# Seven block products instead of eight in half of the down projection's row pairs, with the stationary operands kept in DRAM

## The chip, the cores and the metric

The kernel runs on one core of one Trainium2 chip. The metric is the device time of one execution in microseconds; the time before is the median of three runs. One further execution was recorded by the hardware profiler. Engines: PE multiplies matrices, DVE and ACT work elementwise, POOL is a third elementwise engine that also issues some transfers, SP issues the loads and stores.

## The reference, cut to what matters

One layer of an encoder on 256 tokens of width 2048, all in float32: a mixer with two attention branches, then the MLP at its end:

```python
h = rms_norm(x, norm_mlp_pre[l])
u = jnp.square(jax.nn.relu(jnp.einsum('bsd,df->bsf', h, w_up[l])))      # 2048 -> 8192
x = x + rms_norm(jnp.einsum('bsf,fd->bsd', u, w_down[l]), norm_mlp_post[l])   # 8192 -> 2048
```

The change lies in the last line, the down projection: u is 256 x 8192, w_down is 8192 x 2048.

## The kernel before

Every operand of a large product is split into a high part `hi` (the value rounded to the matmul's float32r format) and a low part `lo` (what is left). A product is three matmuls into the same PSUM bank: hi x hi, hi x lo and lo x hi. ACT makes the high part (a cast), DVE the low part (a subtraction). That is `split`, lines 115 and 116, for weights.

Weights are loaded in pieces of 1 MB by SP's queue into the pool `wp`, which has three buffers each for `raw`, `hi` and `lo`. The loads, the splits and the products are written in program order; a scheduler then decides the order on every engine, and semaphores keep it in step.

The up projection (the loop over `cg`, 16 groups of 512 of the 8192 columns) holds the weights stationary and gives u transposed: `u` is [128 columns, 4, 256 tokens] per group. Its evacuation `u_evac` adds two halves (ACT copy, DVE add, lines 254 and 256), takes the maximum with zero and the scale (line 761), and squares (ACT, line 762). Sixteen tiles `u` stay in SBUF, in the pool `pages` (27 pages of 4 KB per partition).

The down projection holds the activations stationary and lets the weights stream. Its 8192 rows are 64 row tiles `k` of 128. For each, `dweight` loads 128 x 2048 weights and splits them in two halves of 1024 columns, and, once in four row tiles, splits the activations `u` (`usplit`, lines 746 and 747). `dmm` (lines 777 to 779) makes the three matmuls for token tile t (2) and column block c (4 of 512 columns); the eight sums `acc` fill all eight PSUM banks during the whole projection:

```python
for k in range(2, NK - LAST):
    w = dweight(k)
    for t in range(2):
        for c in range(4):
            dmm(k, t, c, w)
```

The last three row tiles go token tile by token tile, so that tile 0 is evacuated while tile 1 is still multiplied. The evacuation squares each bank on ACT with a running sum (line 807), multiplies it with the gain on DVE (line 809), then comes the scale (lines 811, 85, and 88 on POOL) and the output pass with the residual (line 816) with a store (line 819).

Of the kernel before, what the change touches and what calls it, by code (L numbers as in the profile page):

```python
# [17 lines left out]
P = 128  # L18
D = 2048
# [19 lines left out]
def encoder_layer(ctx: ExitStack, tc: tile.TileContext, a, out):  # L39
# [6 lines left out]
    tmp = ctx.enter_context(tc.tile_pool(name="tmp", bufs=6))  # L46
    tiny = ctx.enter_context(tc.tile_pool(name="tiny", bufs=8))
    dram = ctx.enter_context(tc.tile_pool(name="dram", bufs=1, space=bass.MemoryType.DRAM))
    mm = ctx.enter_context(tc.tile_pool(name="mm", bufs=NMM, space=PSUM))
# [22 lines left out]
    def along_tokens(r, b, name):  # L72
        """r [P tokens, token tile] as a row of all tokens, on all partitions."""
# [7 lines left out]
    def inv_rms(ss, n, name, r=None):  # L81
        """(ss / n + eps) ** -0.5, per partition."""
# [9 lines left out]
    last_load = [None]  # L92

    def load(src, k0, nk, c0, cw, name):
        """Rows k0*128.. of a weight: [P, nk, cw]."""
        raw = wp.tile([P, nk, cw], F32, tag="raw", name=f"{name}_w")
        view = src[k0 * P : (k0 + nk) * P, c0 : c0 + cw].rearrange("(k p) c -> p k c", p=P)
        last_load[0] = nc.sync.dma_start(raw, view).ins
# [73 lines left out]
    def advance(n):  # L172
        """Trace the next n stages of the attention heads that wait for their turn, and one chore."""
# [9 lines left out]
    def wgroup(src, c0, act, nk, evac, name, first=(), hook=None, mid=None, after={}, k_first=False, inner=None):  # L183
        """out^T of 512 columns: weights stationary. act(k) is [P, hi 256 | lo 256]."""
# [66 lines left out]
    def halves(ps, name):  # L251
        """The sum of the two halves of a bank, in SBUF."""
# [67 lines left out]
    # Position bias: row (h, i) of rpbp holds the bias of row offset i - 3 at column offsets  # L320
    # -63..63. Each is written 64 times at a pitch of 127 and read at a pitch of 126.
# [52 lines left out]
    def product3(ps, stat, s_at, mov, m_at, start, stop):  # L374
        """ps (+)= stat^T @ mov, each given in two parts."""
# [43 lines left out]
    def p_transposed(p, name):  # L419
        """[P queries, (t, keys)] -> [P keys, (key tile, queries)]"""  # L420
# [320 lines left out]
    ust = {}  # L741

    def usplit(i):
        uh = page([P, 4, T], F32R, f"uh{i}")
        ul = page([P, 4, T], F32R, f"ul{i}")
        nc.scalar.copy(uh, uT[i])
        nc.vector.tensor_sub(ul, uT[i], uh.bitcast(F32))
        ust[i] = (uh, ul)
# [6 lines left out]
    uT = []  # L755
    for cg in range(DFF // 512):
# [8 lines left out]
        uT.append(u)  # L765
        if cg == DFF // 512 - 2:
            usplit(0)

    acc = [[bank(f"acc{t}{c}", t * 4 + c >= 8 - NMM) for c in range(4)] for t in range(2)]
    NK = DFF // P  # L770
    LAST = 3
    def dmm(k, t, c, w):
# [100 lines left out]
```

## Time and profile before

| what | value |
|---|---|
| runs | 1397.62 us median of three (1397.48 to 1398.73) |
| profiled execution, span from first to last instruction | 1394.5 us |
| its own time around the span | not given; the median lies 3.1 us above the span |
| PE, DVE, ACT busy | 1374.6, 835.8, 668.7 us |
| down projection, first to last matmul start | 1037.22 to 1385.18 us |
| 64 loads of `w_down`, 1 MB each | 4.9 us from issue to landing (median) |

A row of a group reads: line, engine, operation, output<-inputs, shape, count | busy time, mean ns of one | idle time of the engine just before them and what ended it. A matmul's duration overlaps the next one's; the pace is read from the starts.

### The profile page before, as it was taken

The page shows a single profiled execution, that of the slowest core. Times are in us where ns is not written, and L with a number is a line of the kernel's source. Part 1 is how long each engine was busy: PE and PEld are TensorE (multiplying, and loading weights), DVE is VectorE, ACT ScalarE, POOL GpSimd, SP SyncE. Part 2 cuts the span into 40 slices and gives each one's busy share as a digit, 9 for nine tenths or more (in the row PEclk, how much of TensorE's full clock was granted, in tenths as well). Part 3 has the DMA queues.
Part 4 walks back from the last instruction along what each step waited for, and adds up shares of the span by engine and source line. Part 5 has one row for each costly group of instructions (what it writes and reads, how often), then busy time and mean ns, then how long its engine had stood idle before and what let it go on. Part 6 is the DMA issues. An engine that isn't in the chain of part 4 may idle for free.

```text
span 1394.5 us, 17896 instructions
## 1 busy us (share of the span) xinstructions
PE 1374.6 (99%) x7240; PEld 1177.8 (84%) x7240; DVE 835.8 (60%) x1155; ACT 668.7 (48%) x1023; POOL 7.9 (1%) x19
## 2 busy tenths in 40 slices
PE   7999999999999999999899999999999999999997
PEld 6888888888888888888788888888888888888886
DVE  6868866676656565654755555555575554444445
ACT  7554554545444445543744444444464543334332
POOL 0000000000000000000000000000000000000000
PEclk9999999999999999999999999999999999999999
DMA  9674755564555555675455565656555556555551
GB/s 317 202 214 154 202 177 173 171 191 155 165 205 182 203 181 183 203 279 184 149 182 181 182 193 170 211 170 200 189 196 185 203 186 227 195 187 205 181 199 73
DMA packets 117490, 265.16 MB, mean 190 GB/s; under 512 B 15008, under 2 KB 16288, under 8 KB 109216
## 3 DMA queue, kind: packets, MB, share of 16 engines
q1 hardware_dynamic: 117264, 264.03, 57.3%
q8 instruction: 56, 0.92, 0.3%
q14 instruction: 26, 0.21, 0.0%
q10 hardware_dynamic: 144, 0.01, 0.0%
HBM read 261.92 MB, written 3.92 MB: 191 GB/s over the span
## 4 chain that ended last, share of the span: by engine, by line
PE 98%; DVE 1%; DMA 0%; ACT 0%; SPq 0%; issue 0%; DVEq 0%; POOLq 0%; POOL 0%; ACTq 0%
PE u_p L191 17%; PE u_p L192 9%; PE acc L779 8%; PE acc L778 8%; PE acc L777 8%; PE gb_p L191 4%; PE ga_p L191 4%; PE qa_p L191 2%; PE gb_p L192 2%; PE ga_p L192 2%; PE ka_p L191 2%; PE qn_p L191 2%; PE bb_p L191 2%; PE ba_p L191 2%; PE kn_p L191 2%; PE y_p L229 2%
## 5 line engine op out<-in xcount | busy, mean ns | idle before, releaser
L191 PE MATMUL u_p<-h2T,u_h 128*128 128x512 f32 x1024 | 359.9, 398 | 0.5 <-DVE r_m L85 0.5
L192 PE MATMUL u_p<-h2T,u_l 128*128 128x256 f32 x1024 | 284.3, 280 | 0.0
L116 DVE TENSOR_TENSOR d_l<-d_w,d_h 128x1024 fp32r<-128x1024 f32 x128 | 151.1, 1221 | 164.2 <-ACT d_h L115 163.7
L116 DVE TENSOR_TENSOR u_l<-u_w,u_h 128x1024 fp32r<-128x1024 f32 x128 | 151.1, 1222 | 146.0 <-ACT u_h L115 144.7
L191 PEld LDWEIGHTS u_p<-h2T,u_h 128*128 128x128 f32 x1024 | 192.0, 189 | 45.5 <-DVE r_m L85 0.9
L115 ACT CAST d_h<-d_w 128x1024 fp32r<-128x1024 f32 x128 | 128.3, 1052 | 191.1 <-PE acc L779 187.5
L778 PE MATMUL acc<-d_l,uh 128*128 128x512 f32 x512 | 199.0, 389 | 0.0
L779 PE MATMUL acc<-d_h,ul 128*128 128x512 f32 x512 | 198.9, 389 | 0.0
L777 PE MATMUL acc<-d_h,uh 128*128 128x512 f32 x512 | 198.2, 389 | 0.0
L192 PEld LDWEIGHTS u_p<-h2T,u_l 128*128 128x128 f32 x1024 | 193.8, 189 | 1.3
L115 ACT CAST u_h<-u_w 128x1024 fp32r<-128x1024 f32 x128 | 128.0, 1049 | 123.9 <-PE u_p L191 62.5
L778 PEld LDWEIGHTS acc<-d_l,uh 128*128 128x128 f32 x512 | 96.1, 188 | 20.1
L777 PEld LDWEIGHTS acc<-d_h,uh 128*128 128x128 f32 x512 | 96.1, 188 | 20.0
L779 PEld LDWEIGHTS acc<-d_h,ul 128*128 128x128 f32 x512 | 96.1, 188 | 19.8
L191 PE MATMUL gb_p<-hT,gb_h 128*128 128x512 f32 x256 | 90.4, 398 | 0.0
L191 PE MATMUL ga_p<-hT,ga_h 128*128 128x512 f32 x256 | 90.0, 397 | 0.0
L192 PE MATMUL gb_p<-hT,gb_l 128*128 128x256 f32 x256 | 71.4, 281 | 0.0
L192 PE MATMUL ga_p<-hT,ga_l 128*128 128x256 f32 x256 | 70.3, 280 | 0.0
L191 PEld LDWEIGHTS gb_p<-hT,gb_h 128*128 128x128 f32 x256 | 47.9, 188 | 11.5
L116 DVE TENSOR_TENSOR gb_l<-gb_w,gb_h 128x1024 fp32r<-128x1024 f32 x32 | 37.8, 1221 | 31.1 <-ACT gb_h L115 31.1
L191 PEld LDWEIGHTS ga_p<-hT,ga_h 128*128 128x128 f32 x256 | 47.4, 188 | 10.5
L116 DVE TENSOR_TENSOR y_l<-y_w,y_h 128x1024 fp32r<-128x1024 f32 x32 | 37.9, 1222 | 27.8 <-ACT y_h L115 27.8
(213 smaller groups left out, 2348.1 us busy)
## 6 DMA issues: line engine op xcount, KB each, us to landing
u_w<-in_w_up SPq DMA_DIRECT2D x64, 1024.0 KB, 5.4
d_w<-in_w_down SPq DMA_DIRECT2D x64, 1024.0 KB, 4.9
ga_w<-in_w_in SPq DMA_DIRECT2D x16, 1024.0 KB, 5.2
gb_w<-in_w_in SPq DMA_DIRECT2D x16, 1024.0 KB, 5.2
y_w<-in_w_out SPq DMA_DIRECT2D x16, 1024.0 KB, 5.1
ka_w<-in_w_in SPq DMA_DIRECT2D x8, 1024.0 KB, 6.1
va_w<-in_w_in SPq DMA_DIRECT2D x8, 1024.0 KB, 5.2
qn_w<-in_w_in SPq DMA_DIRECT2D x8, 1024.0 KB, 5.1
```

Of the source, the lines that this page charges most:

```text
L115: nc.scalar.copy(hi[part], raw[part])
L116: nc.vector.tensor_sub(lo[part], raw[part], hi[part].bitcast(F32))
L191: nc.tensor.matmul(ps[b], hi[:, k % 4, cs], mv, start=(k == 0), stop=False)
L192: nc.tensor.matmul(ps[b][:, :T], lo[:, k % 4, cs], mv[:, :T], start=False, stop=(k == nk - 1))
L229: nc.tensor.matmul(ps[t], sh, hi[:, k % 4], start=(k == 0), stop=False)
L777: nc.tensor.matmul(acc[t][c], uh[:, k % 4, ts_], hi[:, 0, cs], start=(k == 0), stop=False)
L778: nc.tensor.matmul(acc[t][c], uh[:, k % 4, ts_], lo[:, 0, cs], start=False, stop=False)
L779: nc.tensor.matmul(acc[t][c], ul[:, k % 4, ts_], hi[:, 0, cs], start=False, stop=(k == NK - 1))
```

## The change

The down projection is cut anew. A *step* is now two row tiles at a distance of 256 rows (`h` = 0, 1) by 1024 columns (half `g`), so that weights form a matrix of 2 x 2 blocks of 128 x 512, and the activations one of 2 x 2 blocks of 128 x 128 (two row tiles by two token tiles). A load is still 1 MB, in rows of 4 KB. The columns are done in two halves one after the other (`for g in range(2)`); each has 16 groups of 512 rows with two steps each (`j` = 0, 1). In a half, eight banks hold four plain sums and four further sums that are recombined at its end.

Steps of odd groups are *plain*: eight block products, 24 matmuls. Steps of even groups use Winograd's form of Strassen's scheme: *seven* products, 21 matmuls, of sums of blocks. DVE makes four sums of activation blocks after each even group of the up projection (`act_sets`) and four sums of weight blocks for each step (`down_weights`: `dt`, lines 826, 828, 829). Of a seven-product step the raw blocks 1 to 3 (`dh`, `dl`, 128 x 1536) and the sums (`eh`, `el`, 128 x 2048) are split, of a plain step the whole (`dh`, `dl`, 128 x 2048). A seven-product step takes two of the three `hi` and `lo` buffers, a plain one takes one.

The activation parts no longer stay in SBUF. `act_sets` stores them to DRAM from POOL's queue (48 stores, 23 MB), and `act_again` loads them in each column half on SP's queue, right behind the first weight load of their group. In names such as `dl031`, `el100` or `bh010` the digits are the half g, the group, and j (for `bh` and `bl`, the loaded activations, the number of the set). The pool `tmp` is closed ahead of the down projection and its space given to the weight sums. The two gain loads `gp2` now stand ahead of the down projection.

The diff, cut to its core:

```diff
-    def dweight(k):
-        if k % 4 == 0 and k // 4 not in ust:
-            usplit(k // 4)
-        return weight(a["w_down"], k, 1, 0, D, f"d{k}")
+    def act_sets(cg, u):
+        srcs = []
+        if seven_of(cg):
+            a11, a21 = u[:, 0:2, :P], u[:, 0:2, P:]
+            a12, a22 = u[:, 2:4, :P], u[:, 2:4, P:]
+            sums = page([P, 4, 2, P], F32, f"sm{cg}")
+            nc.vector.tensor_sub(sums[:, 0], a21, a22)
+            nc.vector.tensor_sub(sums[:, 1], a11, a21)
+            nc.vector.tensor_sub(sums[:, 2], sums[:, 0], a11)
+            nc.vector.tensor_add(sums[:, 3], a12, sums[:, 2])
...
+            for n, part in (("h", hi), ("l", lo)):
+                kd = dram.tile(shape, F32, name=f"keep{n}{cg}{i}", tag=f"keep{n}{cg}{i}")
+                nc.gpsimd.dma_start(kd, part.bitcast(F32))
+                kept[cg, i, n] = (shape, kd)
+    def act_again(cg, g):
...
+                t = page(shape, F32R, f"b{n}{g}{cg}{i}")
+                nc.sync.dma_start(t.bitcast(F32), kd)
...
+    temps.close()
+    down = ctx.enter_context(tc.tile_pool(name="down", bufs=1, reuse_waits="tile"))
+    wd = a["w_down"].rearrange("(g h j p) c -> p h g j c", h=2, j=2, p=P)
+    def down_weights(g, cg, j):
+        raw = wp.tile([P, 4, 512], F32, tag="raw", name=f"dr{g}{cg}{j}")
+        last_load[0] = nc.sync.dma_start(
+            raw.rearrange("p (h b) c -> p h (b c)", h=2),
+            wd[:, :, cg, j, g * 1024 : (g + 1) * 1024],
+        ).ins
+        n = f"{g}{cg}{j}"
+        h1, l1 = wtile("hi", f"dh{n}"), wtile("lo", f"dl{n}")
+        if not seven_of(cg):
+            nc.scalar.copy(h1, raw)
+            nc.vector.tensor_sub(l1, raw, h1.bitcast(F32))
+            return h1, l1
+        t = down.tile([P, 4, 512], F32, tag="t", name=f"dt{n}", bufs=2)
+        nc.vector.tensor_add(t[:, 0:2], raw[:, 1:3], raw[:, 0:1].to_broadcast([P, 2, 512]))
+        nc.scalar.copy(h1[:, 1:4], raw[:, 1:4])
+        nc.vector.tensor_add(t[:, 2], t[:, 0], raw[:, 2])
+        nc.vector.tensor_add(t[:, 3], t[:, 2], raw[:, 3])
+        nc.vector.tensor_sub(l1[:, 1:4], raw[:, 1:4], h1[:, 1:4].bitcast(F32))
+        h2, l2 = wtile("hi", f"eh{n}"), wtile("lo", f"el{n}")
+        nc.scalar.copy(h2, t)
+        nc.vector.tensor_sub(l2, t, h2.bitcast(F32))
+        return h1, l1, h2, l2
...
+        pr.add(0, stat(0, 0), r, 1, last)
+        pr.add(4, stat(1, 0), t, 0, last)
+        pr.add(6, stat(1, 1), t, 1, last)
+        pr.add(5, stat(1, 2), t, 2, last)
+        pr.add(2, stat(1, 3), r, 2)
+        pr.add(1, stat(0, 1), r, 3)
+        pr.add(3, stat(0, 2), t, 3)
...
+            if g == 0:
+                steps += [n0, s0, n1, s1] if b < NG - 2 else [n0, s0, s1, n1]
+            else:
+                steps += [s0, n0, s1, n1]
...
+                if final:
+                    nc.scalar.copy(c11, pr.ps[0])
+                    nc.vector.tensor_add(c12, c11, pr.ps[5])
+                    nc.vector.tensor_add(c21, c12, pr.ps[6])
+                    nc.vector.tensor_sub(c12, pr.ps[4], c12)
+                    nc.vector.tensor_sub(c22, pr.ps[4], c21)
...
+                eight(pr, sets[cg], j, w, which, end)
+                if end:
+                    nc.vector.tensor_add(z, z, pr.ps[i_])
+                    nc.scalar.activation(sq, z, AF.Square, accum_out=ssd[t][:, c : c + 1])
+                    nc.vector.tensor_mul(z, z, gp2[g][:, half * 512 : (half + 1) * 512])
```

What this makes of the order on DVE is seen at three places. First, in the midst of the down projection before, the low parts of one weight load follow each other, with an activation part now and then:

```order
L747 TENSOR_TENSOR ul7_10135<-u7_7501,uh7_10134 128x1024
L116 TENSOR_TENSOR d7_l_9445<-d7_w_9442,d7_h_9444 128x1024 x2
L116 TENSOR_TENSOR d8_l_9481<-d8_w_9478,d8_h_9480 128x1024 x2
L116 TENSOR_TENSOR d9_l_9513<-d9_w_9510,d9_h_9512 128x1024 x2
L747 TENSOR_TENSOR ul8_10267<-u8_7690,uh8_10266 128x1024
```

Now, in the first column half, two pairs of steps (plain steps 050 and 051, seven-product steps 040 and 041):

```order
L826 TENSOR_TENSOR dt040_9790<-dr040_9786 128x1024
L828 TENSOR_TENSOR dt040_9790<-dt040_9790,dr040_9786 128x512
L829 TENSOR_TENSOR dt040_9790<-dt040_9790,dr040_9786 128x512
L822 TENSOR_TENSOR dl050_9755<-dr050_9752,dh050_9754 128x2048
L830 TENSOR_TENSOR dl040_9789<-dr040_9786,dh040_9788 128x1536
L833 TENSOR_TENSOR el040_9797<-dt040_9790,eh040_9796 128x2048
L826 TENSOR_TENSOR dt041_9863<-dr041_9859 128x1024
L828 TENSOR_TENSOR dt041_9863<-dt041_9863,dr041_9859 128x512
L822 TENSOR_TENSOR dl051_9832<-dr051_9829,dh051_9831 128x2048
L829 TENSOR_TENSOR dt041_9863<-dt041_9863,dr041_9859 128x512
L830 TENSOR_TENSOR dl041_9862<-dr041_9859,dh041_9861 128x1536
```

The sums of a seven-product step (826, 828, 829) stand ahead of, or around, the low part of the plain step (822) that PE multiplies before it. Three pairs later in that half have the last sum (829) behind the step's own 128 x 1536 part (830).

Second, at the start of the down projection DVE had these behind the last up group's halves:

```order
L116 TENSOR_TENSOR d0_l_9217<-d0_w_9214,d0_h_9216 128x1024 x2
L116 TENSOR_TENSOR d1_l_9225<-d1_w_9222,d1_h_9224 128x1024 x2
L256 TENSOR_TENSOR up_s_9160<-u15_p0_9018,up_r_9158 128x256
L256 TENSOR_TENSOR up_s_9174<-u15_p1_9019,up_r_9172 128x256
L761 SCALAR_TENSOR_TENSOR up_s_9160<-up_s_9160,r2b_5461 128x256
```

and now, from the last of these halves on (`up_s` of bank 3), it has:

```order
L257 TENSOR_TENSOR up_s_9438<-u15_p3_9257,up_r_9436 128x256
L798 SCALAR_TENSOR_TENSOR up_s_9438<-up_s_9438,r2b_5461 128x256
L826 TENSOR_TENSOR dt000_9506<-dr000_9502 128x1024
L826 TENSOR_TENSOR dt001_9579<-dr001_9575 128x1024
L774 TENSOR_TENSOR al150_9443<-u15_9253,ah150_9442 128x1024
L828 TENSOR_TENSOR dt000_9506<-dt000_9506,dr000_9502 128x512
L828 TENSOR_TENSOR dt001_9579<-dt001_9579,dr001_9575 128x512
L829 TENSOR_TENSOR dt000_9506<-dt000_9506,dr000_9502 128x512
L829 TENSOR_TENSOR dt001_9579<-dt001_9579,dr001_9575 128x512
L833 TENSOR_TENSOR el000_9513<-dt000_9506,eh000_9512 128x2048
```

The low parts for the first two steps are still made ahead of the halves; the sums of the first seven-product step, and with them `el000`, stand behind them.

Third, at the switch between the column halves, where before there was only the row of `d_l` shown above, DVE now has, from the last plain step of the first half (`dl0151`) to the second half's first sums (`el100`) and the emptying of the banks `p01`, `p02`, `p04` to `p06`:

```order
L822 TENSOR_TENSOR dl0151_10584<-dr0151_10581,dh0151_10583 128x2048
L829 TENSOR_TENSOR dt100_10639<-dt100_10639,dr100_10635 128x512
L830 TENSOR_TENSOR dl100_10638<-dr100_10635,dh100_10637 128x1536
L905 TENSOR_TENSOR zw00_10574<-zw00_10574,p05_9465 128x512
L833 TENSOR_TENSOR el100_10646<-dt100_10639,eh100_10645 128x2048
L906 TENSOR_TENSOR zw01_10575<-zw00_10574,p06_9466 128x512
L915 TENSOR_TENSOR zw00_10574<-zw00_10574,p01_9461 128x512
L826 TENSOR_TENSOR dt101_10716<-dr101_10712 128x1024
L907 TENSOR_TENSOR zw00_10574<-p04_9464,zw00_10574 128x512
L908 TENSOR_TENSOR zw01_10575<-p04_9464,zw01_10575 128x512
L822 TENSOR_TENSOR dl110_10681<-dr110_10678,dh110_10680 128x2048
```

Behind these stand a gain (919), a sum (828) and the pass that empties `p02` (915). The emptying of the banks (905 to 908, 915) is woven into the weight parts.

At the end of the second half the same passes follow the last plain step's part, and the output passes of token tile 0 come only after all of them.

More of the change, by code (lines that the diff above doesn't have):

```diff
@@ new lines, in encoder_layer, with __init__, add @@
+    class Products:
+        def __init__(self, name, low):
+            self.ps = [bank(f"{name}{i}", i in low) for i in range(8)]
+            self.begun = set()
+        def add(self, i, stat, w, blk, last=False):
+            (sh, sl), (wh, wl) = stat, w
+            nc.tensor.matmul(self.ps[i], sh, wh[:, blk], start=i not in self.begun, stop=False)
+            self.begun.add(i)
+            nc.tensor.matmul(self.ps[i], sh, wl[:, blk], start=False, stop=False)
+            nc.tensor.matmul(self.ps[i], sl, wh[:, blk], start=False, stop=last)
@@ new lines, in seven, with stat, eight @@
+    def seven(pr, sets, j, w, last):
+        def stat(i, at):
+            return tuple(part[:, at, j] for part in sets[i])
+        r, t = w[:2], w[2:]
+        pr.add(0, stat(0, 0), r, 1, last)
[5 more added lines that the diff above has]
+        pr.add(3, stat(0, 2), t, 3)
+    PLAIN = ((1, 0, 1), (2, 0, 0), (3, 1, 1), (7, 1, 0))
+    def eight(pr, sets, j, w, which, last):
+        i, t, half = PLAIN[which]
+        for k in (0, 2):
+            stat = tuple(part[:, j + k, t * P : (t + 1) * P] for part in sets[0])
+            pr.add(i, stat, w, k + half, last and k == 2)
@@ L798, in encoder_layer @@
         )
[L799 to L809 removed]
+    zw = {}
@@ new lines, in encoder_layer @@
+    ssd = [small(4, f"ssd{t}") for t in range(2)]
+    for g in range(2):
+        steps = []
+        for b in range(0, NG, 2):
+            s0, s1, n0, n1 = (b, 0), (b, 1), (b + 1, 0), (b + 1, 1)
+            if g == 0:
+                steps += [n0, s0, n1, s1] if b < NG - 2 else [n0, s0, s1, n1]
+            else:
+                steps += [s0, n0, s1, n1]
+        pr = Products(f"p{g}", (0, 4, 5, 6))
+        sets = {}
+        for i, (cg, j) in enumerate(steps):
+            end = i == len(steps) - 1
+            w = down_weights(g, cg, j)
+            if cg not in sets:
+                with tc.issue_after(last_load[0]):
+                    sets[cg] = act_again(cg, g)
+            if seven_of(cg):
+                final = not any(seven_of(c) for c, _ in steps[i + 1 :])
+                seven(pr, sets[cg], j, w, final)
+                if final:
+                    for t in range(2):
+                        zw[g, t] = page([P, 2, 512], F32, f"zw{g}{t}")
+                    c11, c12 = zw[g, 0][:, 1], zw[g, 0][:, 0]
+                    c21, c22 = zw[g, 1][:, 1], zw[g, 1][:, 0]
+                    nc.scalar.copy(c11, pr.ps[0])
[3 more added lines that the diff above has]
+                    nc.vector.tensor_sub(c22, pr.ps[4], c21)
+                continue
+            for which in range(4):
+                eight(pr, sets[cg], j, w, which, end)
+                if end:
+                    i_, t, half = PLAIN[which]
+                    z = zw[g, t][:, half]
+                    nc.vector.tensor_add(z, z, pr.ps[i_])
+                    sq = down.tile([P, 512], F32, tag="junk", name=f"jd{g}{which}", bufs=2)
+                    c = g * 2 + half
+                    nc.scalar.activation(sq, z, AF.Square, accum_out=ssd[t][:, c : c + 1])
+                    nc.vector.tensor_mul(z, z, gp2[g][:, half * 512 : (half + 1) * 512])
```

79 lines of the change are left out of this document (31 added, 48 removed).

## The prediction

> **What bounds the kernel now.** I read the page's busy shares and its chain first.
>
> ```profile
> span 1394.5 us, 17896 instructions
> PE 1374.6 (99%) x7240; PEld 1177.8 (84%) x7240; DVE 835.8 (60%) x1155; ACT 668.7 (48%) x1023; POOL 7.9 (1%) x19
> ...
> PE 98%; DVE 1%; DMA 0%; ACT 0%; SPq 0%; issue 0%; DVEq 0%; POOLq 0%; POOL 0%; ACTq 0%
> ```
>
> PE carries 98% of the chain, so only fewer products, or a stall of PE, can move the time much. The stretches of the up projection and of the down projection show what lies beside PE in each:
>
> ```profile
> core 0: us, PE busy (x) PEld busy (x) DVE busy (x) ACT busy (x) POOL busy (x), PEclk, DMA share, GB/s
> 700.00:1030.00 330.00, 330.00 (x1888) 287.52 (x1887) 183.58 (x239) 158.24 (x238) 0.00 (x0) 1.00 0.58 186
> 1040.00:1384.00 344.00, 344.00 (x1519) 284.87 (x1518) 169.07 (x152) 140.80 (x152) 0.54 (x1) 1.00 0.54 185
> ```
>
> In the down stretch DVE is busy for 49% and the DMA engines for 54%, at full clock. The groups from the end of the up projection on give the durations:
>
> ```profile
> L777 PE MATMUL acc<-d_h,uh 128*128 128x512 f32 x512 | 198.2, 389 | 0.0
> L116 DVE TENSOR_TENSOR d_l<-d_w,d_h 128x1024 fp32r<-128x1024 f32 x128 | 151.1, 1221 | 164.2 <-ACT d_h L115 163.7
> L115 ACT CAST d_h<-d_w 128x1024 fp32r<-128x1024 f32 x128 | 128.3, 1052 | 191.1 <-PE acc L779 187.5 <-issue 3.6
> ...
> L816 DVE SCALAR_TENSOR_TENSOR zw<-zw,rd_r,x 128x512 f32<-128x512 f32 x8 | 5.5, 747 | 0.7 <-POOL rd_r L88 0.7
> L809 DVE TENSOR_TENSOR zw<-acc,gp 128x512 f32<-128x512 f32 x8 | 5.3, 688 | 6.2 <-ACT jd L807 5.9
> L807 ACT ACTIVATE jd<-acc 128x512 f32<-128x512 f32 x8 | 4.7, 596 | 9.8 <-PE acc L779 9.7
> L762 ACT ACTIVATE u<-up_s 128x256 f32<-128x256 f32 x8 | 3.2, 419 | 1.7 <-DVE up_s L761 1.7
> L761 DVE SCALAR_TENSOR_TENSOR up_s<-up_s,r2b 128x256 f32<-128x256 f32 x8 | 3.2, 420 | 0.1
> L256 DVE TENSOR_TENSOR up_s<-u_p,up_r 128x256 f32<-128x256 f32 x8 | 3.2, 419 | 0.0
> L254 ACT COPY up_r<-u_p 128x256 f32<-128x256 f32 x8 | 2.9, 368 | 3.4 <-PE u_p L192 3.4
> ...
> L88 POOL TENSOR_TENSOR rd_r<-rd_m,expo 128x1 f32<-128x1 f32 x2 | 1.1, 540 | 689.6 <-DVE rd_m L85 689.6
> ```
>
> PE never idles there (0.0). The 389 ns of a product overlap the next one; the pace stands in the timeline, from the last product of the up projection to the first and the last of the down projection:
>
> ```profile
> 1037.10 0.28 PE L192 MATMUL u_p<-h2T,u_l 128*128 128x256 f32 x1
> 1037.22 0.39 PE L777 MATMUL acc<-d_h,uh 128*128 128x512 f32 x1
> ...
> 1385.18 0.39 PE L779 MATMUL acc<-d_h,ul 128*128 128x512 f32 x1
> ```
>
> 1536 products start within 347.96 us: 0.2267 us each. The waits say who paces whom:
>
> ```profile
> ACT d_h L115 <- PE acc L779: 187.5, 56, 3.4
> DVE d_l L116 <- ACT d_h L115: 163.7, 57, 3.1
> ...
> SPq L98 <- DVE d_l L116: 290.0, 59, 9.1
> ```
>
> ACT waits for PE to release a weight buffer, DVE for ACT, and the loads for DVE: all run as far ahead as three buffers let them.
>
> **The change part by part.**
>
> *Products.* A plain step (24 products) stays; a seven-product step has 21. 32 such steps lose 3 each: 96 fewer, 96 x 0.2267 = **-21.8 us**, all on the path. A pair of one plain and one seven-product step is 45 products, 10.20 us, where 48 took 10.88.
>
> *Weight parts.* No row has an instruction 1536 or 2048 wide; I extend them. DVE: 688 ns at 512 and 1221 at 1024 give 533 per 512 more, so 1.75 and 2.29 us. ACT, with this row for 512:
>
> ```profile
> L115 ACT CAST qa_h<-first_w 128x512 fp32r<-128x512 f32 x4 | 2.3, 629 | 2.6 <-DMA first_w<-in_w_in 2.6
> ```
>
> 423 ns per 512 more: 1.48 and 1.90 us. DVE has in a pair: 2.29 (plain), and 1.22 + 0.69 + 0.69 (sums), 1.75, 2.29 (parts): 8.9 us. ACT has 5.3. DVE thus goes from 49% to 88% of the time and the cover becomes thin. Where all three sums stand ahead of the plain step's part, or two of them, ACT's cast of the sums (1.90) runs beside DVE's 1.75 or 2.29, and the pair fits into 10.2. In some pairs of the first column half the last sum stands behind the 1.75 part; then DVE sits through that cast: 8.9 + 1.9 + 0.1 = 10.9 us. Three pairs with 0.7 too much, against the 1.1 us that PE has in hand because five products with the high part (5 x 0.2267) come first: **+1 us**, bounds 0 and 2.
>
> *Activations through DRAM.* Per two pairs the queue now carries four weight loads of 1.05 MB, four sets of 0.52 MB each for the sums and the plain group and two of 0.39 MB, 7.1 MB instead of 4.2. What the engines can carry, and how long a load takes:
>
> ```profile
> d_w<-in_w_down SPq DMA_DIRECT2D x64, 1024.0 KB, 4.9
> ...
> gp<-in_g_mlp_post SPq DMA_DIRECT2D x2, 512.0 KB, 5.6
> ```
>
> ```profile
> 10.00:15.00 5.00, 5.00 (x25) 4.44 (x24) 3.53 (x7) 4.90 (x10) 0.00 (x0) 1.00 1.05 393
> ```
>
> At 393 GB/s 7.1 MB take 18.0 us of the two pairs' 20.4: hidden, at 88%. The row is from the start of the kernel, where loads of 0.25 to 1 MB are in flight together as they will be here, so I take it; the other end is below, among the rivals. [...] The stores to DRAM (23 MB from POOL's queue over some 345 us, 67 GB/s on 186) have long landed when they are read, and nobody waits for them: 0, bounds 0 and 1.
>
> *Up projection.* DVE gets 4 sums of 256, parts of 256, 512 and 1024 in eight groups (4.0 us) and 1.22 in eight, 42 us on 56% of 345; 20 us of it were in the down projection before. PE's order there is unchanged, and each chunk's parts are made one or two chunks ahead: 0, bounds 0 and 2.
>
> *Start of the down projection.* In the new order the sums of the first seven-product step stand behind the last group's square and its parts. From the last product of the up projection (U): PE's tail 0.2, copy 0.37, add 0.42, maximum 0.42 = U+1.4; then DVE has 1.22, 1.22, 1.22, 0.69, 0.69, 0.69 = U+7.1 (the first step's sums are done), ACT casts them (1.90, U+9.0), DVE makes the low part (2.29, U+11.3). PE reaches its first product with that low part after 24 + 7 products, U+7.0. Loss **4.2 us**; bounds 2 (instructions without dependence overlap by some 0.1 us) and 6. Under it lies a second lateness: the first set is queued behind four weight loads and two gains, 5.2 MB or 13 us at 393 GB/s, of which two loads go out only in the last 9 us before U (the raw buffers come free with the last chunk's parts). I estimate that it lands up to 2 us after U, within the 4.2.
>
> *The switch between column halves.* Here two seven-product steps stand side by side, the eight banks are emptied and the second half begins. From the low part of the first of the two (about 1 us ahead of its first product) DVE has 2.6, 1.75, 1.22, 2.29, 0.69, 2.29, 0.69, 1.75, 0.69, 2.29 = 16.3 us up to the low part of the second half's first sums; PE has 21 + 21 + 24 products, 15.0 us. So PE starts the half about on time and stands after three products, because the bank of its fourth is emptied only after 0.69, 0.69, 1.22, 0.69, 0.69 more of DVE: 3.7 us lost. Six products later it needs a bank that is emptied after 2.29, 0.69, 0.69, 0.69: 3.0 us lost. Less the overlap, **+6.3 us**, bounds 3 and 9.
>
> *The end.* Before, after the last product:
>
> ```profile
> 1385.66 0.60 ACT L807 ACTIVATE jd<-acc 128x512 f32<-128x512 f32 x1 [1.41 <-PE acc L779]
> ...
> 1386.38 0.69 DVE L809 TENSOR_TENSOR zw<-acc,gp 128x512 f32<-128x512 f32 x1 [1.41 <-ACT jd L807]
> ...
> 1388.05 2.74 DVE L816 SCALAR_TENSOR_TENSOR zw<-zw,rd_r,x 128x512 f32<-128x512 f32 x4 [0.72 <-POOL rd_r L88]
> ```
>
> The last row of output was ready at 1390.8, 5.4 us after the last product. Now token tile 0 no longer finishes ahead of tile 1. DVE makes the last low part some 4.5 us before the end (20 products use it), then has twelve passes of 512 (four recombining, four adding, four with the gain), then the four output passes of tile 0, the scale of tile 1 (with 0.54 on POOL) and the four of tile 1: -4.5 + 12 x 0.67 + 0.4 + 2.74 + 0.85 + 2.74 = 10.3. **+5 us**, bounds 3 and 6.
>
> *Sum.* -21.8 + 1 + 4.2 + 6.3 + 5 = -5.3 us on the profiled span of 1394.5. The median of the runs, 1397.6, lies 3.1 above that span; I carry the same over: **1392.3 us**. All low ends of the costs give -13.8, all high ends +4.2.
>
> **The rivals.**
>
> *The stalls are better covered.* The durations in a row are shorter than their sum (four of 688 ns took 2.65 us), and PE may work off the start's and the switch's hold-ups with products further ahead. Half of both: -10.6 us, 1387.
>
> *Nothing left: the DMA queue paces PE by a little.* In the down stretch above, 185 GB/s go with a share of 0.54, which is 343 GB/s at a full share. If that is what the queue carries, two pairs take 20.6 us and not 20.4; with a wait of 0.1 for each load on top, 16 x 0.3 = 5 us, and the time is 1397. Against it: the share also counts time in which an engine only waits, as the 393 GB/s at 1.05 show. [...]
>
> *Slower: the weight load's latency closes a loop.* In the first half's pairs the load of the next seven-product step goes out only when the plain step's part is made (three raw buffers), and the next plain part stands on DVE behind that load's sums. One turn is the load + 1.22 + 0.69 + 0.69 + 2.29 + 0.2 = load + 5.1 us. It must fit into 10.2, so it decides from a load of 5.1 us on; the row says 4.9 with an idle queue, and 5.6 where the gains were queued behind other loads. With sets ahead of it and 6.0 us, 16 pairs lose 0.9 each: +14 us, 1407. For it: the margin is 0.2 us. Against: in the order of the loads the seven-product step's one goes out when the sets before it have been carried.
>
> *Slower still: DVE and ACT take turns in every pair,* 10.9 instead of 10.2 us: +22 us, 1414. Against it: only a few pairs stand in that order.
>
> **How the numbers follow.** A change under 0.2% (2.8 us) is about what cannot be told from none. The forecast gets 0.42 (own range 1387 to 1395), better cover 0.13, nothing left 0.20, the load's loop 0.17, the turns 0.08. Faster: 0.55; within 0.2%: 0.20; slower: 0.25. The range of 1384 to 1407 takes in the low ends, "nothing left" and the loop, and leaves out the turns and some of the tails.
>
> **What would show it.** Right: 45 products in 10.2 us in a stretch of the first half, PE idle of about 4 us behind the first seven-product step, 6 to 7 us in two pieces at the switch, with DVE's recombining passes as releasers, and 10 to 11 us from the last product to the last output row. Wrong: PE waiting for DVE's plain part in every pair, with DVE in turn waiting for a weight load (the loop) or for ACT's cast (the turns), or loads that take 6 us and more; or, on the other side, a PE without idle at the start and at the switch.

## The result and the profile after

The changed kernel takes 1404.9 us (median of four runs, 1403.1 to 1406.8) where the kernel before took 1398.1 in the same session: a ratio of 1.0054, 95% interval 1.0040 to 1.0068. I had forecast 1392.3 and faster; it is slower. The profiled execution spans 1401.4 us, 6.9 more than before. The page's head, the chain that ended last by engine, and two of the DMA issues (KB each, median us from issue to landing):

```profile
span 1401.4 us, 18140 instructions
PE 1360.9 (97%) x7144; PEld 1162.5 (83%) x7144; DVE 991.4 (71%) x1283; ACT 718.4 (51%) x1009; POOL 33.9 (2%) x67
...
PE 87%; DVE 6%; DMA 5%; ACT 1%; issue 1%; SPq 0%; DVEq 0%; POOLq 0%; POOL 0%; ACTq 0%
...
dr<-in_w_down SPq DMA_DIRECT2D x64, 1024.0 KB, 6.4
bh<-keeph SPq DMA_DIRECT2D x32, 512.0 KB, 8.0
```

96 matmuls are gone, and 11% of the chain has gone from PE to DVE and DMA. What PE waited for in the down projection (us in all, times, the longest):

```profile
PE p L846 <- DMA bh<-keeph: 9.0, 3, 5.6
PE p L848 <- DVE el L833: 6.5, 6, 2.4
PE p L848 <- DVE dl L822: 0.2, 1, 0.2
```

Sets of activations (`bh`) and the low part of weight sums (`el`): nothing of that kind stood there before. The stretches of the start, the switch and the rest of the second half:

```profile
core 0: us, PE busy (x) PEld busy (x) DVE busy (x) ACT busy (x) POOL busy (x), PEclk, DMA share, GB/s
1037.00:1047.00 10.00, 7.26 (x29) 5.64 (x28) 8.36 (x14) 4.64 (x8) 1.06 (x2) 0.83 1.02 395
1208.00:1221.00 13.00, 6.77 (x19) 4.60 (x18) 11.83 (x16) 4.52 (x9) 0.00 (x0) 0.74 1.02 399
1225.00:1368.00 143.00, 137.57 (x602) 112.20 (x601) 115.05 (x79) 68.36 (x41) 0.00 (x0) 1.00 0.85 321
```

The first two also show a granted clock (PEclk) below 1, which the kernel before did not have in its down projection (1.00 from 1037.2 to 1385.5). PE's rows at the switch show why a hole costs more than its length:

```profile
1208.34 0.39 PE L849 MATMUL p<-dh,bl 128*128 128x512 f32 x1
1214.38 0.77 PE L846 MATMUL p<-dh,bh 128*128 128x512 f32 x1 [5.65 <-DMA bh<-keeph]
...
1217.63 0.63 PE L846 MATMUL p<-eh,bh 128*128 128x512 f32 x1
1218.05 0.63 PE L848 MATMUL p<-el,bh 128*128 128x512 f32 x1
...
1221.03 0.40 PE L846 MATMUL p<-dh,bh 128*128 128x512 f32 x1
```

Behind the wait products start 0.43 us apart, not 0.2267. From the first of these rows to the last there are 16 products, 3.6 us of work; they take 12.7, so the switch loses 9.1 us.

The account of the span: products -21.8 (96 x 0.2267); start 2.8 us of waiting and 1.5 at half clock; two waits late in the first half 1.65; switch 9.1; five waits for `el` in the second half 6.2; end +4.4 (13.7 us from the start of the last product to the end of the span, 9.3 before); some 1.4 that is left over, in small waits and pitches a little over 0.2267; and 1.5 because the down projection began 1.5 us later. The last is no cost of the change that I can show: in kernels that are alike up to there the last product of the up projection starts at 1037.55 (e13) or at 1039.43 (e10). So single spans are compared below by the *down stretch*, from the start of the last up product to that of the last down product; 1440 products at 0.2267 would need 326.5 us.

### The profile page after: what moved, and what is told of

Read it like the earlier page. It is cut to its first block, busy times and chain, and to the rows that moved or that the text cites. A ratio compares the mean times of both kernels' runs of the same rounds, so it can differ in the third digit from the quotient of the medians.

```text
span 1401.4 us, 18140 instructions
## 1 busy us (share of the span) xinstructions
PE 1360.9 (97%) x7144; PEld 1162.5 (83%) x7144; DVE 991.4 (71%) x1283; ACT 718.4 (51%) x1009; POOL 33.9 (2%) x67
## 4 chain that ended last, share of the span: by engine, by line
PE 87%; DVE 6%; DMA 5%; ACT 1%; issue 1%; SPq 0%; DVEq 0%; POOLq 0%; POOL 0%; ACTq 0%
PE u_p L192 17%; PE u_p L193 8%; PE p L848 5%; PE p L849 5%; PE p L846 4%; PE gb_p L192 4%; PE ga_p L192 4%; DMA dr<-in_w_down 3%; PE qa_p L192 2%; PE gb_p L193 2%; PE ga_p L193 2%; PE qn_p L192 2%; PE ka_p L192 2%; PE bb_p L192 2%; PE ba_p L192 2%; PE kn_p L192 2%
## 5 line engine op out<-in xcount | busy, mean ns | idle before, releaser
L117 DVE TENSOR_TENSOR u_l<-u_w,u_h 128x1024 fp32r<-128x1024 f32 x128 | 151.1, 1221 | 91.4 <-ACT u_h L116 90.1
L848 PE MATMUL p<-dl,bh 128*128 128x512 f32 x352 | 138.4, 393 | 0.2 <-DVE dl L822 0.2
L849 PE MATMUL p<-dh,bl 128*128 128x512 f32 x352 | 136.7, 391 | 0.0
L846 PE MATMUL p<-dh,bh 128*128 128x512 f32 x352 | 115.7, 393 | 8.4 <-DMA bh<-keeph 8.4
L832 ACT CAST eh<-dt 128x2048 fp32r<-128x2048 f32 x32 | 61.3, 1914 | 78.8 <-DVE dt L829 57.1
L821 ACT CAST dh<-dr 128x2048 fp32r<-128x2048 f32 x32 | 61.2, 1913 | 66.4 <-PE p L849 65.9
L822 DVE TENSOR_TENSOR dl<-dr,dh 128x2048 fp32r<-128x2048 f32 x32 | 73.2, 2287 | 21.1 <-ACT dh L821 20.9
L846 PEld LDWEIGHTS p<-dh,bh 128*128 128x128 f32 x352 | 66.7, 189 | 23.0 <-issue 6.0
L833 DVE TENSOR_TENSOR el<-dt,eh 128x2048 fp32r<-128x2048 f32 x32 | 73.3, 2289 | 14.2 <-ACT eh L832 14.2
L848 PEld LDWEIGHTS p<-dl,bh 128*128 128x128 f32 x352 | 66.8, 190 | 14.8 <-DVE dl L822 0.6
L849 PEld LDWEIGHTS p<-dh,bl 128*128 128x128 f32 x352 | 66.6, 189 | 14.2 <-DMA bl<-keepl 0.4
L117 DVE TENSOR_TENSOR gb_l<-gb_w,gb_h 128x1024 fp32r<-128x1024 f32 x32 | 37.8, 1221 | 31.1 <-ACT gb_h L116 31.1
```

Source lines behind the costliest of these rows:

```text
L117: nc.vector.tensor_sub(lo[part], raw[part], hi[part].bitcast(F32))
L821: nc.scalar.copy(h1, raw)
L822: nc.vector.tensor_sub(l1, raw, h1.bitcast(F32))
L832: nc.scalar.copy(h2, t)
L833: nc.vector.tensor_sub(l2, t, h2.bitcast(F32))
L846: nc.tensor.matmul(self.ps[i], sh, wh[:, blk], start=i not in self.begun, stop=False)
```

## The experiments

| kernel | down stretch, us | median, us | ratio to before (95%) |
|---|---|---|---|
| before | 348.1 | 1398.1 | 1 |
| changed | 349.1 | 1404.9 | 1.0054 (1.0040 to 1.0068) |
| e1 sets earlier at the switch | 349.1 | 1403.1 | 1.0033 (1.0020 to 1.0046) |
| e2 sets earlier at the start | 351.9 | 1405.2 | 1.0060 (1.0048 to 1.0072) |
| e3 second half in the first's order | 348.4 | 1402.6 | 1.0030 (1.0019 to 1.0040) |
| e4 four raw buffers | 338.1 | 1391.1 | 0.9955 (0.9943 to 0.9967) |
| e15 25 pages, three raw buffers | 349.7 | 1402.4 | 1.0042 (1.0029 to 1.0055) |
| e8 sets loaded once | 344.2 | 1396.1 | 0.9994 (0.9984 to 1.0003) |
| e9 PE kept busy at the switch | 347.0 | 1401.9 | 1.0031 (1.0020 to 1.0043) |
| e5 e4, plain steps first at the start | 342.0 | 1394.7 | 0.9980 (0.9971 to 0.9989) |
| e6 e5, plain step first at the switch | 340.4 | 1393.9 | 0.9975 (0.9966 to 0.9984) |
| e10 e4, sets kept over the switch | 342.6 | 1395.9 | 0.9989 (0.9980 to 0.9998) |
| e11 e10, sets kept at the start | 340.5 | 1393.2 | 0.9971 (0.9959 to 0.9982) |
| e13 e10, DVE's order at the switch | 334.8 | 1387.3 | 0.9925 (0.9913 to 0.9938) |
| e16 e13 and e11's start | 328.7 | 1381.7 | 0.9886 (0.9869 to 0.9902) |

### Second half: what closes the loop

The chain of work in the changed kernel through one turn of the second half (start, duration, what):

```profile
1263.14 5.05 DMA dr<-in_w_down
...
1273.15 0.50 PE p L848
...
1280.02 0.24 PE p L849
...
1280.28 1.92 ACT dh L821
...
1282.23 2.30 DVE dl L822
...
1284.55 6.79 DMA dr<-in_w_down
...
1291.36 1.24 DVE dt L826
...
1293.95 2.29 DVE el L833
...
1296.29 0.50 PE p L848
```

Read from top to bottom this is a ring: 7.1 us after PE has got the low part of one step's sums it frees a `hi` buffer; ACT casts the plain step's weights into it (1.92); DVE makes their low part (2.30), which frees a raw buffer; a weight load goes out (6.79); DVE makes the sums of the *next* seven-product step from it, then the low part `el` for which PE waits, and PE can go on. This `el` needs nothing of that load. The timeline shows it:

```profile
1288.76 1.91 ACT L832 CAST eh<-dt 128x2048 fp32r<-128x2048 f32 x1 [4.50 <-DVE dt L829]
...
1291.36 1.22 DVE L826 TENSOR_TENSOR dt<-dr 128x1024 f32<-128x1024 f32 x1 [2.71 <-DMA dr<-in_w_down]
...
1293.34 0.69 DVE L829 TENSOR_TENSOR dt<-dt,dr 128x512 f32<-128x512 f32 x1
1293.95 2.28 DVE L833 TENSOR_TENSOR el<-dt,eh 128x2048 fp32r<-128x2048 f32 x1
```

Its high part `eh` was done at 1290.67, and PE needed `el` at about 1293.7. But in DVE's order the next step's three sums stand ahead of it; DVE stood 2.71 us for their load and began `el` only at 1293.95. The load closes the ring through DVE's order. From one wait to the next are 23.14 us, 6.79 of them the load: the rest is 16.35. Two pairs are 20.4 us of products, so this ring, with this order on DVE, holds PE up as soon as the load takes more than 4.05 us. With the 5.05 us of the first row it gives 21.4, one us too much, which is the spacing of the next waits (1296.29, 1317.81, 1339.15, 1360.73).

**e3.** The step order of the second half only; its first two steps stay:

```diff
-            if g == 0:
+            if b == 0 and g:
+                steps += [s0, n0, n1, s1]
+            else:
                 steps += [n0, s0, n1, s1] if b < NG - 2 else [n0, s0, s1, n1]
-            else:
-                steps += [s0, n0, s1, n1]
```

> The second column half takes its steps from the second pair of groups on in the order of the first half (plain, seven, plain, seven; the last pair plain, seven, seven, plain). Nothing else is moved. In the changed kernel PE waits five times in the second half for the sums' low part, 6.2 us in all, once in every two pairs of steps. Theory 1 (the loop of weight load, sums and low part closes because of the order in which the second half takes its loads and DVE its passes): these waits go, the second half runs as the first (10.2 us a pair), 5 to 6 us faster, about 1399. Rival 2 (the loads are slow because weights and sets share the queue, 6.4 us against 4.9 before, whatever the order): 5 to 6 us stay lost, within 1 us of the changed kernel.

The second half's waits shrank from 6.2 to about 2.3 us, but the down stretch by only 0.7, since the steps of the first half, unchanged, lost some 3 us more in this execution than in the changed kernel's. The median is 0.24% below the changed kernel's, with intervals that just touch (seven runs, 1398.4 to 1403.5 us). The order matters, and mends part of it only: inconclusive as to size.

**e4.** A fourth raw buffer (the same `bufs=4` in the other two places that make a raw tile), paid for with two pages:

```diff
-    pages = ctx.enter_context(tc.tile_pool(name="pages", bufs=27))
+    pages = ctx.enter_context(tc.tile_pool(name="pages", bufs=25))
...
-        raw = wp.tile([P, 4, 512], F32, tag="raw", name=f"dr{g}{cg}{j}")
+        raw = wp.tile([P, 4, 512], F32, tag="raw", name=f"dr{g}{cg}{j}", bufs=4)
```

> The changed kernel with four raw weight buffers instead of three (two pages fewer, 25 instead of 27, to make room). At the switch the sets then stand behind five weight loads. Theory 1 (the second half's waits come from the three raw buffers: a load goes out only when the buffer of three steps before is free): the five waits of 6.2 us go, and the switch loses 1 to 4 us more than the changed kernel's 9, its set being queued behind one load more; in sum 2 to 5 us faster, about 1401. Rival 2 (the queue itself is the limit): the waits of the second half stay at 5 to 6 us, and with the switch the kernel is 1 to 4 us slower, about 1407. Up projection and before: 0 to 2 us from the two pages less.

**e15.** The pages alone.

> The changed kernel with 25 pages instead of 27 and three raw buffers as it has: the other half of the edit in e4. Theory 1 (e4's 13 us come from the fourth raw buffer): as the changed kernel, 1403 to 1406, with the waits for the sums' low part in the second half. Rival 2 (the pages made the difference, by when the sets can be loaded): 5 us faster or more.

e15 is as the changed kernel; e4 is 1.0% faster than the changed kernel and 0.45% faster than the kernel before. More than I expected, because the two waits late in the first half went too and the switch did not get worse. All that PE waits for in e4's down projection are sets, once at the start and twice at the switch (the 2.9, put down to ACT's `ah`, is the wait of the down projection's first product; in the changed kernel that product started at 1041.61, before its own `ah` was done at 1041.78, so I take it for the set's wait here too):

```profile
PE p L846 <- DMA bh<-keeph: 4.4, 2, 3.8
PE p L846 <- ACT ah L773: 2.9, 1, 2.9
```

The loads did not get shorter (7.3 us against 6.4): the fourth buffer lets them go out earlier. DVE's own waits for weight loads, 22.3 us in 14 pieces in the changed kernel's down projection, are gone altogether, though in e4's second half too every second `el` stands behind the next seven-product step's first two sums. So the number of buffers closes the ring, and not the queue's capacity. The scheduler wrote DVE's passes in a somewhat different order here; what that alone is worth wasn't separated.

**e8.** From the second pair of each half on the first pair's sets are used again, so the queue carries 4.2 MB in two pairs instead of 7.1 (this leaves the other groups' activations out):

```diff
-                    sets[cg] = act_again(cg, g)
+                    sets[cg] = act_again(cg, g) if cg < 2 else sets[cg % 2]
```

> The changed kernel with three raw buffers, but in each half only the first pair's sets are loaded from DRAM and all later steps use these again (this leaves the activations of the other groups out). The queue then carries 4.2 MB in two pairs instead of 7.1. Theory 1 (three raw buffers and a load close a loop; its length hangs on the load's duration): the weight load falls from 6.4 to about 5 us, the five waits of the second half shrink by 1.4 us each to under 1 us in all; 5 us faster than the changed kernel, about 1400. Rival 2 (what closes the loop is the buffers and DVE's order alone): the load gets shorter, and the waits stay; within 1 us of the changed kernel. The start and the switch lose what they lost.

With three raw buffers still, all waits for `el` are gone; a few for `dl` (3.5 us) and those at start and switch stay:

```profile
PE p L846 <- DMA bh<-keeph: 7.7, 2, 5.0
PE p L848 <- DVE dl L822: 3.5, 4, 1.2
PE p L846 <- DVE zw L915: 0.6, 1, 0.6
```

0.6% faster than the changed kernel. The median load fell only to 6.1 us over the whole and from 7.0 to 6.4 in the second half, less than I had said, and more than the 4.05 us of the ring above. So shorter loads are not shown to have opened it: in this kernel `el` also came to stand ahead of the next step's sums on DVE, and DVE still waits 26.7 us in all for weight loads. The chain behind the last wait for `dl` is another loop, over one pair: load, sums, the plain step's low part, load.

```profile
1324.63 5.46 DMA dr<-in_w_down
...
1332.71 2.30 DVE dl L822
...
1335.02 4.94 DMA dr<-in_w_down
...
1342.58 2.29 DVE dl L822
```

One turn is 10.39 us, 4.93 of them beside the load, against 10.2 us of products: this is the loop that I had among the rivals, with 5.1 there.

### Start and switch: what lies under a late set

**e1.** In the second half's first four steps a weight load is issued behind the sets called for before it, so the first sets go out behind one weight load, not four.

```diff
+        with tc.issue_after(last_set[0]) if last_set[0] else nullcontext():
+            last_load[0] = nc.sync.dma_start(
...
+            if g == 0 or i > 3:
+                last_set[0] = None
```

> At the switch of column halves the six loads of the second half's first sets go out right behind the first of the four weight loads (and the next two weight loads behind the sets), instead of behind all four. Nothing else is moved. In the changed kernel PE stands 5.8 us there for a set, 1.6 us more in small waits, and then runs about 8 us at half clock (some 2 us lost): 9 us in all. Theory 1 (the order of the queue makes the set late; once the set is there, the emptying of the banks by DVE, which I had forecast as 6.3 us, comes in its place): the wait for a set goes, PE waits twice for DVE's recombining passes, 2 to 3 us each, no half clock; 5 to 6 us remain of 9, the kernel is 3 to 4 us faster than the changed one, about 1401. Rival 2 (the set is all there is, the banks are empty in time): 8 to 9 us faster, about 1396. Rival 3 (the queue is full there, so the set lands late in any order): 0 to 1 us, about 1404.

```profile
1213.94 0.50 PE L849 MATMUL p<-eh,bh 128*128 128x512 f32 x1 [1.03 <-DVE zw L913]
1218.95 1.21 PE L849 MATMUL p<-dh,bh 128*128 128x512 f32 x4 [1.53 <-ACT dh L824]
1221.28 0.67 PE L851 MATMUL p<-dl,bh 128*128 128x512 f32 x1 [1.11 <-DVE dl L825]
```

No wait for a set any more; instead PE waits for a bank that DVE empties late, and then for the next step's parts, whose load now stands behind the sets. With half clock behind them (granted 0.83 in 1220 to 1230) 6.0 us are lost, 3.1 less than 9.1 (theory 1: 5 to 6 left). The amount is near the forecast's 6.3 us, but by chance: only the first of the three waits, 1.2 us of the 6.0, has the releaser I had named. The median is 1.8 us lower, with intervals that overlap, and the down stretch of this execution is as long as the changed kernel's, in part because a wait in the second half was followed by half clock (last section).

**e2.** The same at the start, and the two gain loads eight steps later.

> At the start of the down projection the first sets go out behind the first and second weight load, ahead of the third and fourth, and the two gain loads 8 steps later. Nothing else is moved. In the changed kernel PE stands 2.8 us there for the first set and runs 4.3 us at half clock (some 1.5 to 2 us lost). Theory 1 (the forecast's term of 4.2 us lies under it: the first seven-product step's sums are ready only at 11 us after the last up product, which was 1038.6, so at about 1049.7, and PE would be there at 1046): the wait for the set goes and a wait of 3 to 4 us for the low part of the sums comes in its place; 0 to 1 us faster, about 1404. Rival 2 (the set was the only hold-up): 4 us faster, about 1401.

```profile
1045.85 0.50 PE L851 MATMUL p<-dl,bh 128*128 128x512 f32 x1 [1.84 <-DVE dl L833]
1048.38 1.20 PE L849 MATMUL p<-eh,bh 128*128 128x512 f32 x4 [0.87 <-ACT eh L835]
1050.71 0.50 PE L851 MATMUL p<-el,bh 128*128 128x512 f32 x1 [0.91 <-DVE el L836]
```

PE starts its first product at once (1037.93) and then loses 4.1 us in three holes, on the parts and sums for which I had forecast 4.2. Nothing is gained: theory 1 holds. (The down stretch is 2.8 us longer than the changed kernel's, by waits further on.)

**e9.** 22 unused products while PE waits at the switch:

```diff
+        if g == 1:
+            x = sets[NG - 1][0][0]
+            with tc.issue_after(last_mm[0]):
+                for _ in range(22):
+                    nc.tensor.matmul(pr.ps[0], x[:, 0, :P], x[:, 0:2], start=True, stop=True)
```

> The changed kernel; while PE waits for the set at the switch it makes 22 products (5.0 us) whose result nobody uses, into the bank that the first product of the second half starts anew. Theory 1 (the half clock behind the wait comes from PE's idle time): the granted clock stays whole, the products behind it have a pitch of 0.23 us instead of 0.43, some 2 us faster than the changed kernel. Rival 2 (the half clock comes from elsewhere): pitch 0.43 for 7 us as before, 0 us. If the set comes earlier than the 22 products end, up to 0.5 us is lost to them.

```profile
1208.00:1221.00 13.00, 11.96 (x52) 9.26 (x51) 13.00 (x16) 5.24 (x10) 0.00 (x0) 1.00 1.01 401
```

The granted clock is 1.00 where it was 0.74, and the products have their full pitch. From the first product behind the wait to the last of the rows shown above the changed kernel takes 6.65 us, e9 5.01 (1216.01 to 1221.02), with much the same small waits in between: the half clock alone cost 1.6 us here. Theory 1 holds. (The set also came at least 0.8 us earlier after the first half's last product; the medians differ by 0.23%, with intervals that overlap a little.)

**e5 and e6.** Four raw buffers, sets earlier at start and switch, the first pair's order n0, n1, s0, s1 (n plain, s seven); e6 also begins the second half with a plain step.

> Four raw buffers (1391.1 us, e4), and both other holes mended: at the start the two plain steps of the first pair of groups come first, their set is loaded behind the first weight load, the gains later (so 48 products stand ahead of the first product with sums); at the switch the sets go out behind the first weight load, as in e1. With e4 the start lost 3.0 us of waiting and some 1.4 us at half clock, the switch 5.0 us of waiting and some 2 us at half clock. Theory 1 (the start is covered by 10.9 us of plain products; at the switch DVE's emptying takes the set's place, 4 to 5 us): 4.4 + 2.5 us faster than e4, about 1384. Rival 2 (two seven-product steps side by side in the first pair cost DVE 6.6 us each on 4.8 us of products, so 1 to 4 us come back as waits for low parts): about 1387. Rival 3 (the set is late in any order): as e4, 1391.

> As the start-plain-first kernel (e5), but the second half begins with its plain step and keeps the order plain, seven, plain, seven, so that 48 plain products stand in a row at the switch while DVE recombines. Theory 1 (what is left at the switch is DVE's work in too few products; with 48 of them in a row the waits there are under 1 us): 3 to 5 us faster than e5, about 1380. Rival 2 (the second half's first plain products use the banks that the first half's last plain products leave, so PE waits for four additions of 0.68 us there, and the last pair with two seven-product steps side by side costs 1 to 2 us at the end): within 1.5 us of e5.

Both are slower than e4 (e6 with an interval that just meets e4's), and my theories for both fell. At the start the plain products covered the set, but waits of 0.8 to 1.8 us for `dl`, `el`, `eh` and `dh` (5 us in all, and half clock behind the last, granted 0.83 in 1060 to 1070) took the set's place: the weight loads now stood behind sets. At the switch e5 has e1's three waits again, and e6 has three others of 1.1 to 1.4 us a few us later. Here, putting sets ahead of weights on one queue only changed which of them was late.

**e10 and e11.** So take bytes off the queue. e10: the second half begins with groups 14 and 15, whose sets are still on the chip. e11: the first half begins with 12 and 13, whose sets are kept from the up projection, plain steps first. The order of the pairs (e10 has the second half's alone):

```diff
-        for b in range(0, NG, 2):
+        for b in ([NG - 4, *range(0, NG - 4, 2), NG - 2] if g == 0 else [NG - 2, *range(0, NG - 2, 2)]):
```

> Four raw buffers (1391.1 us, e4); the second half begins with the last pair of groups (14 and 15), whose sets are still on the chip, so nothing has to come from DRAM before the first products and the queue has 2.9 MB less to carry at the switch. In e4 the switch loses 5.0 us of waiting (3.8 for the set) and some 2 at half clock. Theory 1 (my forecast's term: DVE empties the banks only between the parts of the steps around; in e4's trace the bank of the fourth product was free at 1212.4, 6 us behind the first half's last product): the wait for the set turns into a wait for a recombining pass, 4 to 6 us at the switch, 0 to 2 us faster than e4, about 1390. Rival 2 (with the set there the switch is covered): 6 to 7 us faster, about 1384.5.

> As the kernel before (e10), and the first half begins with groups 12 and 13, whose sets stay on the chip from the up projection, with their two plain steps first (then the pairs 0 to 10, then 14). In e4 the start loses 3.0 us of waiting for a set and some 1.5 at half clock. Theory 1 (sets there, 48 plain products ahead of the sums): PE starts right behind the up projection, waits of 1 to 2 us for low parts, 3 us faster than e10. Rival 2 (DVE makes the first sums behind the last up group's square whatever is loaded, and two seven-product steps follow each other, so 4 to 6 us of waits stay, as with the plain steps first in e5, 5.4 us): within 1 us of e10.

In e10 the switch has 3.6 us of waits left, for `dl` and for a bank, without half clock (granted 1.00 from 1200 to 1230; theory 1: 4 to 6; the bank's part is 1.5), and e11's start has none at all (0.18% better than e10, with intervals that overlap a little; theory 1's 3 us). Yet e10 is 0.3% slower than e4, because a ring closed again in its second half, five times 1.1 to 1.5 us, now over `dl`:

```profile
PE p L849 <- DVE dl L823: 6.8, 6, 1.5
PE p L847 <- DMA bh<-keeph: 3.1, 1, 3.1
PE p L847 <- DVE zw L916: 1.4, 1, 1.4
```

Its chain goes as in the changed kernel (ACT 1.92, DVE 2.29 and 1.77, load 7.28, DVE 2.29). Here the plain step's `dl` stands behind the first sum of the next seven-product step on DVE, and DVE waits 15.4 us in six pieces for that sum's load; in e4 it waits for none. Four raw buffers are no cure by themselves; why the loads come late again in e10 and not in e4 I didn't isolate.

**e13.** e10 with DVE's queue in another order: recombining passes ahead of the next steps' parts, products with the gain three steps later, the one pair of adjacent seven-product steps moved to the middle of the first half.

```diff
+            low_behind[0] = emptied[0] if g == 1 and i == 0 else None
+            with tc.issue_after(emptied[0]) if g == 1 and i in (1, 2) else nullcontext():
+                w = down_weights(g, cg, j)
...
+            elif g == 0 and b == 6:
+                steps += [n0, s0, s1, n1]
```

> As e10, with DVE's work at the switch put in another order: the first half's four recombining passes ahead of the second half's first sums' low part and of the parts of its next two steps; the four products with the gain three steps later; and the one place where two seven-product steps stand side by side moved from the end of the first half to its middle (pairs 0 to 4 plain first, pair 6 in between, the others seven first). Theory 1 (DVE's order is what is left at the switch): 1 to 3 us lost there instead of 5 to 7, no half clock: 4 us faster than e10, about 1386 or less. Rival 2 (DVE has 33 us of work in these steps' 25 us of products, in whatever order): within 1 us of e10.

0.64% faster than e10: the switch keeps two waits, 1.9 us, with half clock behind them (granted 0.83 in 1210 to 1220), and the second half has none. Three orders were changed at once, so which of them did it is open.

**e16.** e13 and e11's start.

> The kernel with DVE's work at the switch in another order (e13, 1387.3 us, four raw buffers, last pair's sets carried over the switch) with the start of e11 in addition: the first half begins with groups 12 and 13, whose sets stay on the chip, plain steps first. In e13 the start loses 3.0 us of waiting for a set and some 1.7 at half clock; in e11 PE had no wait behind the up projection. Theory 1 (the start's loss is the set and the sums, and both are covered): 4 to 5 us faster than e13, about 1383. Rival 2 (in e11 the hold-up was only pushed on: the two seven-product steps side by side leave DVE behind for the first half, and the second half's phase of weight loads and splits comes out as in e10 and e11, five to seven waits of 1.2 us): within 1 us of e13, about 1387.

```profile
span 1380.6 us, 18139 instructions
PE 1355.7 (98%) x7144; PEld 1160.3 (84%) x7144; DVE 990.5 (72%) x1283; ACT 718.9 (52%) x1009; POOL 34.0 (2%) x67
...
PE 97%; DVE 1%; ACT 1%; DMA 0%; issue 0%; SPq 0%; DVEq 0%; POOLq 0%; POOL 0%; ACTq 0%
```

1381.7 us, 1.1% faster than the kernel before and 0.4% (5.6 us) than e13, so theory 1 holds. All that is left of the waits:

```profile
PE p L852 <- ACT dh L826: 0.8, 2, 0.6
PE p L852 <- ACT dh L832: 0.2, 1, 0.2
```

The down stretch is 328.7 us, 2.2 above the products' own 326.5: the start's and the switch's losses are taken away beside each other, not pushed on. Of the 21.8 us of products the kernel keeps 15.8; what is missing is mostly these 2.2 us and the end, 3.5 us longer than before in this execution.

## Why the prediction was wrong

By its own steps, on the profiled span (forecast 1389.2, measured 1401.4, 12.2 more):

- **Products, -21.8:** right. e16 shows it whole: 19.4 us less in the down stretch than before, 2.2 of stalls left.
- **Durations of the wider passes:** right to 0.02 us (1.75 and 2.29 on DVE; ACT 1.91 against 1.90).
- **Pairs with the last sum late, +1:** 1.65, three quarters through the first half, and near the size partly by luck. The chain into these waits goes through two such pairs as I had described them (10.55 and 10.57 us, where I had 10.9), and then through a weight load of 6.19 us, which the term didn't have; e4, without any wait of DVE for a load, has none of them.
- **Activations through DRAM, hidden at 88%: the step that failed.** The queue carried the bytes (395 to 399 GB/s in the stretches of start and switch, as the 393 I had taken), and "nothing left" as a matter of capacity fell with e4. But the 0 us in the sum counted bytes only, and left out the load's *latency*, 4.9 us before. It became 6.4, and in the second half 4.9 to 9.7. I had a loop as a rival, with a chance of 0.17, in the first half, over one pair, as load + 5.1 us. Such a loop exists (e8, 4.93), but the first half loses to a load no more than the 1.65 above. The ring that cost 6.2 us runs over two pairs, in the second half's order of steps: through PE's release of a `hi` buffer, ACT's cast, the raw buffer and the load, and through DVE's order, in which `el` stands behind the next step's sums, as load + 16.35 us against 20.4. A fourth raw buffer (e4) takes it away, and the two pages it costs don't (e15).
- **Switch, +6.3:** 9.1. The mechanism that ended last was another: six sets queued behind four weight loads, of which the last waited for a raw buffer. What I had named is there, but smaller: with the sets on the chip (e10) 3.6 us are lost, 1.5 of them on a bank that DVE empties late, where I had two such waits of 3.7 and 3.0. The half clock, 1.6 us of the 9.1 (e9), was in no term.
- **Start, +4.2:** 4.3, by the same accident: the set landed 2.6 us after the up projection's end ("up to 2 us, within the 4.2"), and half clock made up the rest. What I had named was real too (e2: 4.1), and hidden behind the set.
- **End, +5:** +4.4, about as worked out. From the end of the last product (1388.06) to the last output row the chain takes 9.3 us where I had 10.3:

```profile
1390.42 0.69 DVE zw L919
...
1391.18 2.65 DVE zw L927 x4
...
1396.03 1.32 DVE zw L927 x2
```

  It is read from the chain; no run took it away.
- **The rest:** 1.4 us of small pitches, and 1.5 by the later start of the down projection.

The kernel before cannot gain what e4 gains: its 1536 down products follow one another at 0.2267 us without a wait. A run of it with four raw buffers wasn't tried.

## What to carry to other kernels

When a change puts more on a queue that hides its loads, ask not only whether the bytes fit but how long a turn each buffer makes: follow one buffer from its release through every engine to the product that needs it and back, add the load's latency under the new traffic, and compare it with the products in that many steps. Ask also which passes stand behind the one that waits for the load on the same engine: here the costliest wait of that kind was for a part that didn't need the load at all. When two hold-ups lie over each other, removing the upper one shows the lower (e2), and reordering one queue can make something else late (e1, e5, e6); what helped was bytes not loaded, buffers that let loads go out sooner, and DVE's order, tried together. Look at the granted clock behind a wait of PE too: here it was 0.83 over 10 us with a wait of 2.8 us (start) or 2.4 us (e1) in them.

## What the hardware showed that I had not expected

In these runs a stall of PE of about 3 us at the start is followed by products at about half the rate: 0.43 us apart instead of 0.2267, for about 3.4 us (a wait of 2.8 us; granted clock 0.83 in 1037 to 1047) and, after 5.8 us, nearly 6 at the switch (0.74 in 1208 to 1221). It doesn't hang on the wait's length alone. The wait in the second half at 1296, 2.4 us long in both kernels, left the changed kernel at full clock (first row) and e1 not (second row):

```profile
1290.00:1300.00 10.00, 7.56 (x33) 5.90 (x33) 8.57 (x6) 5.39 (x4) 0.00 (x0) 1.00 0.92 355
1290.00:1300.00 10.00, 7.64 (x28) 5.88 (x27) 8.19 (x6) 4.33 (x3) 0.00 (x0) 0.83 0.96 373
```

In e1's switch three waits of 1.0 to 1.5 us within 9 us did the same: 0.43 us apart from 1221.75 to 1224.73, a granted clock of 0.83 in 1220 to 1230. What decides whether half clock follows a wait was not shown by these runs.
